# Six PSUM banks in turn, instead of two, for the input products of the first two chunks

## The chip, the cores and the metric

The kernel runs on one core of one Trainium2 chip. The core has a matrix engine (PE, TensorE; its weight loads are the row PEld), a vector engine (DVE), a scalar engine (ACT), a general engine (POOL) and a queue engine (SP) that issues most of the transfers. Each engine works through its own instructions strictly in the order in which they stand in its queue; an instruction waits on semaphores until what it reads is written and what it overwrites is no longer needed. Matrix results land in PSUM, of which this kernel uses eight banks of 128 x 512 float32: one result of 128 x 512 fills one bank, and the bank can take the next result only when DVE or ACT have read the old one.

The metric is the device time of the core in microseconds (us). The kernel before takes 1899.47 us (median of three runs, 1899.46 to 1902.62).

## The reference

The input x has 2048 positions and 1024 channels. Layer 0 is a gated short convolution, layer 1 is stick-breaking attention with 8 heads of 64 channels, and the output is normalised once more. Cut to what matters:

```python
h = _rmsnorm(x, norm_a)                                # mixer (layer 0)
b_gate, c_gate, xin, g = split(h @ w_in, 4)            # w_in: 1024 x 4096
y = b_gate * causal_depthwise_conv(c_gate * xin, w_conv)   # width 3
x = x + (y * silu(g)) @ w_out
k, v = split(_rmsnorm(x, norm_kv) @ w_kv, 2)           # shared keys and values
q, g = split(_rmsnorm(x, norm_b) @ w_in_b, 2)          # layer 1
o = stick_breaking_attention(q, k, v)                  # strictly causal
x = x + (o * silu(g)) @ w_out_b
out = _rmsnorm(x, norm_f)
```

## The kernel before

**Tiling.** The positions are cut into four chunks of 512 (numbered 0 to 3) and the channels into eight blocks of 128. Everything is held transposed, channels on partitions. Each float32 operand of a big product is split into a high part and a low part, and one product of 1024 channels (`mm3`, L202) is 8 x 3 = 24 matmuls of 128 x 128 by 128 x 512, all at line L208, that accumulate into one bank.

**The stage that is changed.** `mixer_in` (L282) computes the products of the mixer's input projection. It is called as `mixer_in((0, 1))` for the first two chunks together and then as `mixer_in((2,))` and `mixer_in((3,))`. For each of the eight column blocks `cb`, and within it for each chunk `c`, it makes four products: C, X, B and G, with tile names pC, pX, pB, pG. What follows each of them on ACT, DVE and POOL:

- pC is copied by ACT to `cs` (L314);
- pX times `cs` gives `p` on DVE (L321), which is scaled by the squared norm factor (L327);
- three convolution steps make `cv` (ACT L334, DVE L335, L337), and DVE multiplies it by pB (L339) and the norm factor (L346);
- pG is scaled (DVE L344), passed through a sigmoid (ACT L345) and multiplied into `cv`, once as the sigmoid (L349) and once as itself (L350); SP stores `cv` to `y_d` (L351).

So pB's bank is free after L339 and pG's bank after L350. The norm factors of the first two chunks are found late, while their first products already run: `rstd` (L119) sums the squares with small matmuls into a bank of its own (`pst`, tag `st`, one buffer), and `bcast` (L143) spreads the result with two matmuls into the same bank (`prb`), from which ACT makes `rs` (L252, L254).

**The banks.** The eight banks are fixed shares of one pool, by tag: `lin` has 2 (L110), `z` 2, `wt` 2, `av` 1 and `st` 1 (L23). Buffers of a tag are reused in turn. All input products take `lin`, but for pB and pG of the very first column block of chunk 0, which take `z`. The attention (`attention`, L466) uses `z` for the scores, `wt` for the transposed weights and `av` for its output.

**Weights.** `load_w` (L183) loads 128 columns of a weight (`wr_`, 512 KB), lets ACT and DVE split them into high and low (`whl_`, L174 and L175), and stores the split form (`sw_`, 1 MB) for the later chunks. There are four `whl` buffers and two raw ones; a weight is split once the same weight of the previous column block has been used by both chunks.

**What runs beside it.** In the same stage `stats_x` (L259) sums the squares of chunks 2 and 3, and `fold_gains` (L355) multiplies `w_kv` and `w_in_b` by their norm gains, in 32 halves: load (L363), DVE multiply (L364), split on ACT (L174) and DVE (L175), two stores (L367), all in the engines' same queues.

**The order.** Python generators yield estimated costs, and `merge` (L672) interleaves the streams by them. A scheduler then puts every engine's instructions in an order of its own by a timeline that it computes when the kernel is built; so a change of buffers can move instructions on every engine. After the first two chunks' mixer follow the output projection and the projections of chunk 0 (`proj_out` L372, products po, then pk, pq, pv, pg) beside the mixer of chunk 2, the attention of chunk 0 and so on; at the end the attention of chunk 3 runs beside the last projections (`out_b`, `out_norm`, `out_b_last`).

Of the kernel before, what the change touches and what calls it, by code (L numbers as in the profile page):

```python
# [8 lines left out]
F32 = mybir.dt.float32  # L9
# [5 lines left out]
P = 128  # L15
# [4 lines left out]
CH = 512  # L20

NR, NW, NT, NL, NWB, NRAW, NA, NWTS = 5, 8, 4, 5, 4, 2, 16, 2
NLIN, NZ, NWT, NAV = 2, 2, 2, 1  # L23
# [22 lines left out]
def kernel(  # L46
# [18 lines left out]
    psum = ctx.enter_context(tc.tile_pool(name="psum", bufs=2, space=bass.MemoryType.PSUM))  # L65
# [43 lines left out]
    def lin(nm):  # L109
        return psum.tile([P, CH], F32, name=nm, tag="lin", bufs=NLIN)  # L110
# [8 lines left out]
    def rstd(acc, nm, y=None):  # L119


        acc = acc if isinstance(acc, (list, tuple)) else [acc]
        ps = st(f"pst_{nm}")
        for j in range(4):
            for i, a in enumerate(acc):
                nc.tensor.matmul(ps[:, j:j + 1], a[:, j * P:(j + 1) * P], ones[:, 0:1], start=i == 0, stop=i == len(acc) - 1)
        v = sb.tile([P, 4], F32, name=f"v_{nm}", tag="sv")
        nc.vector.tensor_scalar(out=v, in0=ps[:, 0:4], scalar1=1.0 / D, scalar2=EPS, op0=ALU.mult, op1=ALU.add)

        if y is None:  # L130
            y = sb.tile([P, 4], F32, name=f"yr_{nm}", tag="sy")
        t = sb.tile([P, 4], F32, name=f"t_{nm}", tag="st")
        nc.vector.tensor_scalar(out=t.bitcast(I32), in0=v.bitcast(I32), scalar1=1, scalar2=None,
                                op0=ALU.logical_shift_right)
        nc.vector.tensor_scalar(out=y.bitcast(I32), in0=t.bitcast(I32), scalar1=-1, scalar2=0x5F3759DF,
                                op0=ALU.mult, op1=ALU.add)
        for _ in range(3):
            nc.vector.tensor_mul(t, y, y)
            nc.vector.scalar_tensor_tensor(out=t, in0=t, scalar=-0.5, in1=v, op0=ALU.mult, op1=ALU.mult)
            nc.vector.scalar_tensor_tensor(out=y, in0=t, scalar=1.5, in1=y, op0=ALU.add, op1=ALU.mult)  # L140
        return y
# [41 lines left out]
    def load_w(src, key, nm, kt=KD, eng=nc.vector):  # L183

        if key not in split_d:
            wt = w_tile(nm, kt)
            raw = sb.tile([P, kt, P], F32, name=f"wr_{nm}", tag="wraw", bufs=NRAW)
            nc.sync.dma_start(out=raw, in_=src.rearrange("(k p) n -> p k n", p=P))
            split(wt[:, 0], wt[:, 1], raw, eng)
            split_d[key] = dram.tile([P, 2, kt, P], F32, name=f"sw_{nm}")  # L190
            nc.sync.dma_start(out=split_d[key], in_=wt.bitcast(F32))
            return wt
        wt = w_tile(nm, kt)
        nc.sync.dma_start(out=wt.bitcast(F32), in_=split_d[key])
        return wt
# [29 lines left out]
    def norm_x_late(c, between=None):  # L225

        hc, xs = [], []
        for k in range(KD):
            if k == 1 and between is not None:
                between()  # L230
            tag, bufs = (("w", NW), ("R", NR) if k < NR else ("ld", NL))[c]
            x = sb.tile([P, CH], F32, name=f"xh_{c}_{k}", tag=tag, bufs=bufs)
            nc.sync.dma_start(out=x, in_=xT[k * P:(k + 1) * P, cols(c)])
            xs.append(x)
            ga = gains["a"][:, k:k + 1]
            hk = act_tile(f"h_{c}", k)
            nc.scalar.activation(hk[:, 0, :], x, AF.Copy, scale=ga)
            nc.vector.scalar_tensor_tensor(out=hk[:, 1, :], in0=x, scalar=ga, in1=hk[:, 0, :].bitcast(F32),
                                           op0=ALU.mult, op1=ALU.subtract)
            hc.append(hk)  # L240
        return hc, xs

    def squares(c, xs):
        acc = sb.tile([P, CH], F32, name=f"acc_h{c}", tag="acc", bufs=2)
        for k, x in enumerate(xs):
            square_into(acc, x, k == 0, f"h{c}{k}", nc.gpsimd, early=True)
        return acc
# [20 lines left out]
    def norm_x(c):  # L268
        hc = []
        pb = bcast(rx[c], f"hb{c}")  # L270
        for k in range(KD):
            x = load_x(c, k, "n")
            nc.vector.scalar_tensor_tensor(out=x, in0=x, scalar=gains["a"][:, k:k + 1], in1=pb,
                                           op0=ALU.mult, op1=ALU.mult)
            hc.append(act_tile(f"h_{c}", k))
            split(hc[k][:, 0, :], hc[k][:, 1, :], x)
        return hc

    h = {}
    late_acc, late = {}, {}  # L280

    def mixer_in(cs):  # L282
        if len(cs) == 1:
            h[cs[0]] = norm_x(cs[0])
            yield YN * 24 * MM
        for cb in range(KD):
            wts = {}
            for c in cs:
                nm = f"{cb}_{c}"

                def w_src(i):
                    return w_in_a[0][:, i * D + cb * P: i * D + (cb + 1) * P]

                def gate(g, i):
                    if c not in h:
                        if c == 0:
                            load_first = lambda: wts.update({g: load_w(w_src(i), (g, cb), f"{g}{cb}_{cs[0]}")})
                            h[c], late_acc[c] = norm_x_late(c, load_first)
                        else:
                            h[c], xs = norm_x_late(c)  # L300
                            late_acc[c] = rstd(squares(c, xs), f"h{c}")
                    if g not in wts:
                        wts[g] = load_w(w_src(i), (g, cb), f"{g}{cb}_{cs[0]}")
                    if c == cb == 0 and g in "BG":

                        ps = psum.tile([P, CH], F32, name=f"p{g}_{nm}", tag="z", bufs=NZ)
                    else:
                        ps = lin(f"p{g}_{nm}")
                    yield from mm3(ps, wts[g], h[c])
                    return ps  # L310

                pc = yield from gate("C", 1)
                cps = t512(f"cs_{nm}")
                nc.scalar.copy(cps, pc)  # L314
                yield rest(24)
                if c == cb == 0:
                    wts["X"] = load_w(w_src(2), ("X", cb), f"X{cb}_{cs[0]}")
                    late_acc[c] = rstd(squares(c, late_acc[c]), f"h{c}")
                px = yield from gate("X", 2)
                p = sb.tile([P, CH + 2], F32, name=f"p_{nm}", tag="p", bufs=2)  # L320
                nc.vector.tensor_mul(p[:, 0:CH], px, cps)  # L321
                pB = None
                if c in late_acc:
                    if c not in late:
                        pB = yield from gate("B", 0)
                        late[c] = late_rms(c, late_acc[c])
                    nc.vector.tensor_mul(p[:, 0:CH], p[:, 0:CH], late[c][1])  # L327
                nc.gpsimd.tensor_copy(p[:, CH:CH + 2], halo[:, cb, :])
                nc.gpsimd.tensor_copy(halo[:, cb, :], p[:, 0:2])
                yield rest(24)  # L330
                if pB is None:
                    pB = yield from gate("B", 0)
                t = t512(f"cv_{nm}")
                nc.scalar.activation(t, p[:, 0:CH], AF.Copy, scale=cw[:, 2, cb:cb + 1])  # L334
                nc.vector.scalar_tensor_tensor(out=t, in0=p[:, 1:CH + 1], scalar=cw[:, 1, cb:cb + 1], in1=t,  # L335
                                               op0=ALU.mult, op1=ALU.add)
                nc.vector.scalar_tensor_tensor(out=t, in0=p[:, 2:CH + 2], scalar=cw[:, 0, cb:cb + 1], in1=t,  # L337
                                               op0=ALU.mult, op1=ALU.add)
                nc.vector.tensor_mul(t, t, pB)  # L339
                yield rest(24)  # L340
                pG = yield from gate("G", 3)
                sg = t512(f"sg_{nm}")
                if c in late:
                    nc.vector.tensor_mul(sg, pG, late[c][0])  # L344
                    nc.scalar.activation(sg, sg, AF.Sigmoid)  # L345
                    nc.vector.tensor_mul(t, t, late[c][1])  # L346
                else:
                    nc.scalar.activation(sg, pG, AF.Sigmoid)
                nc.vector.tensor_mul(t, t, sg)  # L349
                nc.vector.tensor_mul(t, t, pG)  # L350
                nc.sync.dma_start(out=y_d[c][cb], in_=t)  # L351
                yield rest(24)
# [400 lines left out]
```

## Time and profile before

| what | value |
|---|---|
| median of three runs | 1899.47 us |
| the profiled execution: its time | 1899.87 us |
| the profiled execution: its span, first to last instruction | 1898.2 us |
| mean granted PE clock | 0.975 |
| PE busy | 1787.5 us (94%) |
| PEld busy | 1453.6 us (77%) |
| DVE busy | 1264.4 us (67%) |
| ACT busy | 771.9 us (41%) |
| POOL busy | 433.3 us (23%) |
| data moved | 443.65 MB, mean 234 GB/s |

Three views are used below. The **windows** view gives, for stretches of the span, the busy time of each engine with the number of instructions, then the granted PE clock (1.00 is full), the mean busy share of the DMA engines and GB/s. The **timeline** gives instructions in order of time: start, duration, engine, line, operation, output<-inputs, forms and count; where an engine stood idle before the instruction, a bracket gives the idle time and what ended it. The **waits** view sums these idle times by instruction and releaser. Matmuls are pipelined, so their durations overlap: 24 matmuls read as 5.60 us although the next product starts 5.44 us after them. Times between starts are therefore used. Some records may be missing.

### The profile page before, as it was taken

The numbers are of one execution on the slowest core, as the hardware profiler recorded it, in microseconds if no ns is written. First come the engines' busy times: TensorE is split into PE (matmuls) and PEld (weight loads), VectorE is DVE, ScalarE is ACT, GpSimd is POOL, SyncE is SP. The second block draws the span as 40 slices with busy tenths as digits, with TensorE's granted clock in tenths as the row PEclk, the third lists the DMA queues.
The fourth block names the chain that finished last, engine by engine and source line by source line (L and its number), as shares of the span: only waits on it lengthen the run. The fifth ranks groups of instructions, "written<-read, shape, count | busy, mean of one in ns | idle before, by whom it ended". The sixth has DMA issues, their size and how long they took to land.

```text
span 1898.2 us, 24937 instructions
## 1 busy us (share of the span) xinstructions
PE 1787.5 (94%) x8312; PEld 1453.6 (77%) x8312; DVE 1264.4 (67%) x1927; ACT 771.9 (41%) x1497; POOL 433.3 (23%) x822
## 2 busy tenths in 40 slices
PE   7999999999999999999999999999989999888784
PEld 5777888888888878888888888888857777766563
DVE  7766533564133273538886437787996989999996
ACT  6323211231122132325453324444564666566553
POOL 5100000101011031202222102223231323654651
PEclk9999999999999999999999999999989999999797
DMA  9989855697888778776767776656838565777751
GB/s 291 313 293 311 301 154 163 198 355 252 292 270 283 225 261 266 243 266 204 266 214 264 236 253 202 202 191 197 253 104 266 178 195 175 251 252 252 236 170 50
DMA packets 233871, 443.65 MB, mean 234 GB/s; under 512 B 17936, under 2 KB 132624, under 8 KB 209168
## 3 DMA queue, kind: packets, MB, share of 16 engines
q1 hardware_dynamic: 173664, 383.31, 60.1%
q10 hardware_dynamic: 59920, 58.74, 10.7%
q8 instruction: 66, 1.08, 0.2%
q14 instruction: 61, 0.50, 0.1%
q0 software_dynamic: 160, 0.02, 0.1%
HBM read 314.34 MB, written 127.66 MB: 233 GB/s over the span
## 4 chain that ended last, share of the span: by engine, by line
PE 68%; DVE 17%; DMA 6%; issue 5%; ACT 2%; POOL 1%; SPq 0%; ACTq 0%; POOLq 0%; DVEq 0%
PE pX L208 8%; PE pB L208 7%; PE po L208 7%; PE pC L208 7%; PE pG L208 7%; DVE R L501 5%; PE pv L208 4%; PE pk L208 4%; PE wt L513 4%; PE pq L208 4%; PE pg L208 4%; DVE w L505 3%; PE av L523 3%; DVE wtl L175 2%; PE av L522 2%
## 5 line engine op out<-in xcount | busy, mean ns | idle before, releaser
L501 DVE TENSOR_TENSOR_SCAN R<-R,R,ones 128x512 f32<-128x512 f32 x192 | 259.2, 1352 | 23.5 <-ACT R L490 23.2
L490 ACT ACTIVATE R<-z 128x512 f32<-128x512 f32 (+1 forms) x320 | 174.2, 545 | 171.5 <-DVE R L501 80.5
L175 DVE TENSOR_TENSOR wtl<-wt,wth 128x512 fp32r<-128x512 f32 (+1 forms) x320 | 186.2, 600 | 60.7 <-ACT wth L174 60.1
L174 ACT CAST wth<-wt 128x512 fp32r<-128x512 f32 (+1 forms) x320 | 160.6, 528 | 153.2 <-PE wt L513 134.1
L505 DVE TENSOR_TENSOR w<-w,R 128x512 f32<-128x512 f32 (+1 forms) x320 | 209.2, 661 | 16.1 <-POOL R L500 0.5
L208 PE MATMUL pC<-h,whl_C 128*128 128x512 f32 x768 | 193.3, 401 | 14.4 <-ACT whl_C L174 8.2
L208 PE MATMUL pX<-h,whl_X 128*128 128x512 f32 x768 | 188.4, 395 | 5.9 <-DVE cv L350 5.9
L208 PE MATMUL po<-y,whl_o 128*128 128x512 f32 x768 | 187.8, 392 | 0.0
L208 PE MATMUL pB<-h,whl_B 128*128 128x512 f32 x768 | 185.5, 391 | 0.0
L208 PE MATMUL pG<-h,whl_G 128*128 128x512 f32 x768 | 185.0, 391 | 0.0
L500 POOL COPY R<-R 128x1 f32<-128x1 f32 x192 | 103.9, 541 | 349.3 <-DVE R L501 302.2
L208 PEld LDWEIGHTS pC<-h,whl_C 128*128 128x128 f32 x768 | 146.4, 193 | 48.5 <-ACT whl_C L174 8.2
L513 PE MATMUL wt<-ident,w 128*128 128x128 f32 x1088 | 178.5, 279 | 4.3 <-DVE w L505 3.2
L492 ACT ACTIVATE w<-z 128x512 f32<-128x512 f32 (+1 forms) x320 | 171.9, 542 | 6.5 <-PE wt L513 6.5
L208 PEld LDWEIGHTS pX<-h,whl_X 128*128 128x128 f32 x768 | 143.9, 189 | 37.3 <-issue 3.6
L523 PE MATMUL av<-wtl,vv 128*128 128x512 f32 (+1 forms) x320 | 128.9, 405 | 41.5 <-DVE wtl L175 40.1
L208 PEld LDWEIGHTS po<-y,whl_o 128*128 128x128 f32 x768 | 143.1, 188 | 30.2 <-ACT y L174 0.4
L208 PEld LDWEIGHTS pB<-h,whl_B 128*128 128x128 f32 x768 | 143.4, 188 | 29.6
L208 PEld LDWEIGHTS pG<-h,whl_G 128*128 128x128 f32 x768 | 143.3, 188 | 29.7 <-DVE sgb L443 0.2
L513 PEld LDWEIGHTS wt<-ident,w 128*128 128x128 f32 x1088 | 139.7, 144 | 33.1 <-issue 4.2
L501 DVE TENSOR_TENSOR_SCAN R<-R,ones 128x512 f32<-128x512 f32 (+3 forms) x128 | 116.8, 918 | 36.0 <-POOL R L496 32.5
L487 PE MATMUL z<-kt,q 128*128 128x512 f32 (+1 forms) x320 | 129.9, 408 | 7.3 <-ACT w L492 7.1
(170 smaller groups left out, 2676.9 us busy)
## 6 DMA issues: line engine op xcount, KB each, us to landing
whl_o<-sw_o SPq DMA_DIRECT2D x24, 1024.0 KB, 6.1
kt<-k_d ACTq DMA_DIRECT2D x80, 256.0 KB, 4.0
vv<-v_d ACTq DMA_DIRECT2D x80, 256.0 KB, 4.2
whl_C<-sw_C SPq DMA_DIRECT2D x16, 1024.0 KB, 5.9
whl_X<-sw_X SPq DMA_DIRECT2D x16, 1024.0 KB, 5.4
whl_B<-sw_B SPq DMA_DIRECT2D x16, 1024.0 KB, 5.5
whl_G<-sw_G SPq DMA_DIRECT2D x16, 1024.0 KB, 5.3
whl_k<-sw_kv SPq DMA_DIRECT2D x16, 1024.0 KB, 5.6
```

The costliest lines, as they stand in the source:

```text
L174: nc.scalar.copy(hi, src)
L175: eng.tensor_sub(lo, src, hi.bitcast(F32))
L208: ins = nc.tensor.matmul(ps, w[:, k, :], a[k][:, m, :], start=n == 0, stop=n == 3 * kt - 1)
L487: nc.tensor.matmul(ps[:, lom:CH], q2[:, 0, qi * P:(qi + 1) * P], kt[:, lom:CH], start=True, stop=False)
L490: nc.scalar.activation(R[:, lo + 1:CH + 1], ps[:, lo:CH], AF.Sigmoid, scale=-0.125)
L492: nc.scalar.activation(w[:, lo:CH], ps[:, lo:CH], AF.Sigmoid, scale=0.125)
L500: nc.gpsimd.tensor_copy(R[:, 0:1], carry[qi])
L501: nc.vector.tensor_tensor_scan(out=R[:, lo + 1:CH + 1], data0=R[:, lo + 1:CH + 1], data1=ones[:, 0:1].to_broadcast([P, CH - lo]), initial= ...
L505: nc.vector.tensor_mul(w[:, lo:CH], w[:, lo:CH], R[:, lo:CH])
L513: nc.tensor.transpose(wt[:, qi * P:(qi + 1) * P], ws[qi][:, kb * P:(kb + 1) * P], ident)
L522: nc.tensor.matmul(av[:, 0:n], vs, wh[:, 0:n], start=first, stop=False)
L523: ins = nc.tensor.matmul(av[:, 0:n], vs, wl[:, 0:n], start=False, stop=final)
```

## The change

Every input product of the stage for two chunks takes its bank by a running count: `lin`, `z`, `wt`, `lin`, ... and, as each tag has two buffers, a bank comes round again after six products. The special case of the first column block is dropped. The mixers of chunks 2 and 3 keep `lin`.

```diff
     late_acc, late = {}, {}
+    turn = [0]
...
                         wts[g] = load_w(w_src(i), (g, cb), f"{g}{cb}_{cs[0]}")
-                    if c == cb == 0 and g in "BG":
-
-                        ps = psum.tile([P, CH], F32, name=f"p{g}_{nm}", tag="z", bufs=NZ)
+                    if len(cs) > 1:
+
+                        tag, bufs = (("lin", NLIN), ("z", NZ), ("wt", NWT))[turn[0] % 3]
+                        turn[0] += 1
+                        ps = psum.tile([P, CH], F32, name=f"p{g}_{nm}", tag=tag, bufs=bufs)
                     else:
                         ps = lin(f"p{g}_{nm}")
```

The code behind the change stands three lines further down in the new kernel (L350 becomes L353). The lines named here and in the prediction are those of the kernel before.

The order in which the instructions stand on each engine moves with it. PE's order changes in its first 170 groups of matmuls only slightly: a few matmuls of the first block's products are interleaved otherwise, the two `prb` matmuls of chunk 1 now stand after the first six matmuls of the second block's pC instead of before them, and the `pst` sums of chunks 2 and 3 stand up to two blocks later. From there on PE's order is the same up to the attention of the last two heads of chunk 3, the last 270 groups, which are partly interleaved otherwise. DVE, ACT and SP differ through the first five column blocks and then again only in that last part; POOL only in that last part. In the mixer's stage the DVE, ACT and SP queues hold the fold work later: in front of the last step (L350) of chunk 0 in the second block stand six folds' multiplications, not nine. In the last part ACT holds five scalings of an output (`x2r`, L595) further ahead, SP issues the loads of `sga` and `ogr` (L548, L553) further ahead, and DVE the splits of `og` (L175).

## The prediction

> **What bounds the kernel now.** I read the windows of the whole span first, to see where PE, the busiest engine, is not full.
>
> ```profile
> 60.00:230.00 170.00, 159.49 (x689) 130.53 (x688) 108.37 (x179) 49.19 (x73) 7.22 (x16) 0.97 0.91 312
> 230.00:390.00 160.00, 160.00 (x707) 132.51 (x706) 70.62 (x96) 35.26 (x46) 9.06 (x16) 1.00 0.57 177
> 390.00:1400.00 1010.00, 1000.04 (x4789) 829.39 (x4788) 596.18 (x932) 367.11 (x760) 182.98 (x457) 1.00 0.74 244
> 1780.00:1898.00 118.00, 82.07 (x358) 60.77 (x356) 97.98 (x158) 58.88 (x113) 46.89 (x56) 0.85 0.41 131
> ```
>
> From 230 to 1400 us PE sets the pace: 1160 of 1170 us busy, at full clock. Between 60 and 230, inside the changed stage, it loses 10.5 us and some clock. At the end DVE is the fuller engine. The waits of PE between 60 and 230 name what it lacked:
>
> ```profile
> PE pX L208 <- DVE cv L350: 5.9, 3, 3.2
> PE pC L208 <- DVE cv L339: 3.1, 1, 3.1
> PE pst_h L126 <- ACT rs L254: 1.5, 1, 1.5
> ```
>
> L350 and L339 read nothing that pX or pC uses as input; they are the last readers of pG's and pB's banks. These are waits for one of the two `lin` banks; the third is a wait for the `st` bank, which `rs` still reads. The timeline of PE shows their places and what a product takes otherwise:
>
> ```profile
> 62.64 0.63 PE L157 MATMUL prb_h<-dg_h,onesr 128*128 128x512 f32 x2
> 64.82 1.05 PE L126 MATMUL pst_h<-ones,acc_h 128*128 128x1 f32 x8 [1.55 <-ACT rs L254]
> 68.98 8.25 PE L208 MATMUL pC<-h,whl_C 128*128 128x512 f32 x24 [3.11 <-DVE cv L339]
> 77.07 5.60 PE L208 MATMUL pX<-h,whl_X 128*128 128x512 f32 x24
> ...
> 116.10 5.60 PE L208 MATMUL pC<-h,whl_C 128*128 128x512 f32 x24
> 124.90 7.34 PE L208 MATMUL pX<-h,whl_X 128*128 128x512 f32 x24 [3.20 <-DVE cv L350]
> 132.08 5.60 PE L208 MATMUL pB<-h,whl_B 128*128 128x512 f32 x24
> ...
> 164.72 5.60 PE L208 MATMUL pC<-h,whl_C 128*128 128x512 f32 x24
> 171.93 5.69 PE L208 MATMUL pX<-h,whl_X 128*128 128x512 f32 x24 [1.62 <-DVE cv L350]
> 177.46 5.60 PE L208 MATMUL pB<-h,whl_B 128*128 128x512 f32 x24
> ...
> 210.10 5.60 PE L208 MATMUL pC<-h,whl_C 128*128 128x512 f32 x24
> 216.74 5.72 PE L208 MATMUL pX<-h,whl_X 128*128 128x512 f32 x24 [1.04 <-DVE cv L350]
> 222.30 5.60 PE L208 MATMUL pB<-h,whl_B 128*128 128x512 f32 x24
> ...
> 380.06 5.60 PE L208 MATMUL pG<-h,whl_G 128*128 128x512 f32 x24
> 385.50 5.61 PE L208 MATMUL po<-y,whl_o 128*128 128x512 f32 x24
> ```
>
> The last two rows give 5.44 us from product to product (385.50 - 380.06). Four times the stream breaks, always at a block's first or second product, and after the two longer breaks the next product is slow too. From 222 us on no break is left until the stage ends at 385.50.
>
> **The change part by part.** *Removed, the bank waits.* With six banks a product needs the bank of the product six places back. PE then reaches it five products, 5 x 5.44 = 27.2 us, after that one ended, where it was 5.44 us. Why L350 is late I read in DVE's and ACT's timeline:
>
> ```profile
> 120.41 0.69 DVE L364 TENSOR_TENSOR fold_kv<-fold_kv,g_kv 128x512 f32<-128x512 f32 x1 [3.06 <-DMA fold_kv<-in_w_kv_dram]
> 121.02 0.68 DVE L344 TENSOR_TENSOR sg<-pG,rs 128x512 f32<-128x512 f32 x1
> 124.07 0.69 DVE L350 TENSOR_TENSOR cv<-cv,pG 128x512 f32<-128x512 f32 x1
> ```
>
> pG's results were there at 116.10, when the next product began, yet their first reader L344 stands in DVE's queue behind a fold that waits for its load. pG is free at 124.76, 8.66 us after it ended: too late for 5.44 us, early for 27.2. The four breaks, by starts:
>
> - First: 68.98 - 62.64 = 6.34 us, in which prb and pst stand too. Their own cost, which stays, is 0.47 and 0.81 us, from the starts in the rows below. That leaves 5.06. The slow pC took 77.07 - 68.98 = 8.09, that is 2.65 over 5.44.
> - Second: pC should end at 116.10 + 5.44 = 121.54; 124.90 is 3.36 later. pX took 132.08 - 124.90 = 7.18, 1.74 over.
> - Third: 171.93 - 170.16 = 1.77, and 0.09 over in pX.
> - Fourth: 216.74 - 215.54 = 1.20, and 0.12 over.
>
> ```profile
> 390.95 0.62 PE L157 MATMUL prb_hb<-dg_hb,onesr 128*128 128x512 f32 x2
> 391.42 16.50 PE L208 MATMUL po<-y,whl_o 128*128 128x512 f32 x72
> ...
> 446.97 0.95 PE L126 MATMUL pst_x<-ones,acc_x 128*128 128x1 f32 x8
> 447.78 4.61 PE L208 MATMUL pG<-h,whl_G 128*128 128x512 f32 x19
> ```
>
> Waits 5.06 + 3.36 + 1.77 + 1.20 = 11.39, slow products 2.65 + 1.74 + 0.09 + 0.12 = 4.60, together **-15.99 us**. The `st` wait is in it because pst no longer stands between prb and the reading of `rs`, while six matmuls of pC now cover prb's inputs. The price of moving prb: chunk 1's `rs`, and with it its first L327 and the split of whl_G behind it in ACT's queue, come later by the 14 matmuls that now start before prb ends, 14 x 5.44 / 24 = 3.2 us; that eats into the cover below and nothing else.
>
> The slow products are clock: the granted clock was 0.78 and 0.83 in the two windows that hold them.
>
> ```profile
> 70.00:80.00 10.00, 10.00 (x36) 8.03 (x35) 6.50 (x19) 2.37 (x4) 0.00 (x0) 0.78 1.05 356
> 120.00:130.00 10.00, 6.80 (x23) 5.14 (x22) 5.70 (x8) 3.19 (x5) 0.00 (x0) 0.83 1.06 369
> ```
>
> The Trainium skill ("TensorE: Matmul & The Clock Gate", section "Why this matters for your kernels") says that a PE gap of more than about 3 us brings the clock down to half. By that rule the 4.4 us of the first two slow products go away with their gaps, and the 1.77 and 1.20 us gaps cost no clock, as 0.09 and 0.12 show. If the clock fell for another reason, the gain would be 11.4 us and the sum 4.6 us higher.
>
> *What must now keep up: weights.* A product also needs its split weight, and the queues that make it hold the folds too. I set the splits' ends against the products that use them, in the congested block and in a quiet one:
>
> ```profile
> 116.13 1.22 DVE L175 TENSOR_TENSOR whl_B<-wr_B,whl_B 128x1024 fp32r<-128x1024 f32 x1
> 240.44 1.23 DVE L175 TENSOR_TENSOR whl_C<-wr_C,whl_C 128x1024 fp32r<-128x1024 f32 x1 [4.20 <-ACT whl_C L174]
> 254.94 5.60 PE L208 MATMUL pC<-h,whl_C 128*128 128x512 f32 x24
> ```
>
> Quiet: ready at 241.67, used at 254.94, 13.3 us early. Congested: whl_B ready at 117.35, used at 132.08, which is 126.98 once the second break's 5.10 us are gone: 9.6 us early. So folds and transfers delay a split by up to 3.7 us today, of 13.3. Moving the folds back in the order (six, not nine, ahead of L350 in the second block) helps this. Transfers: the stage's bytes stay, so 312 GB/s over 170 us become 312 x 170 / 154 = 344 GB/s; the queue has carried 369 in the window above. I cost the weights at nothing, with 9.6 us of cover; if it is used up, every us more is one of PE's.
>
> *Before 57 us* PE waits for the first inputs; the new interleaving only swaps matmuls that are ready. Nothing. *The banks of the attention*: its first z matmul runs at 514.10, so the tags are free. *From 385 to 1780 us* order and work stay the same, and the rows above show no wait on anything but the core's own progress, so the whole is shifted.
>
> ```profile
> 514.10 0.39 PE L487 MATMUL z<-kt,q 128*128 128x512 f32 x1
> ```
>
> *The last part is reordered.* DVE's work there is the same, and DVE has little to win:
>
> ```profile
> 1780.00:1860.00 80.00, 64.57 (x297) 49.87 (x295) 77.32 (x115) 46.25 (x91) 40.62 (x51) 0.91 0.54 167
> ```
>
> 80 - 77.32 = 2.7 us idle, the bound of a gain. For a loss I take the scalings L595, which in the new order stand ahead of a sigmoid L490 that ran at 1799.92 and feeds the next scan:
>
> ```profile
> 1794.40 11.12 SPq L594 DMA_DIRECT2D x2r<-y_d  x5
> 1799.92 0.60 ACT L490 ACTIVATE R<-z 128x512 f32<-128x512 f32 x1 [0.26 <-PE z L488]
> 1808.77 0.79 ACT L595 ACTIVATE x2r<-x2r,g_f 128x512 f32<-128x512 f32 x1
> ```
>
> If the fifth scaling ended as late as now, 1809.56, the sigmoid would come 9.6 us later: the bound of a loss. But the loads also wait for buffers that the og splits free, and those move forward in the same order, so most of this should not happen. I take +1.0, near the idle time's end of the range.
>
> **Sum.** Against the profiled execution: 1899.87 - 15.99 + 1.0 = 1884.9. That execution is 0.40 over the median of the runs, so **1884.5 us**. Its own range is 1880.8 (tail -2.7) to 1889 (clock not regained, or tail +5.5).
>
> **Rivals.**
>
> *The weights take half of it.* DVE no longer holds PE back, so its backlog of folds reaches the splits, and the second to fourth breaks come back as waits for whl. For it: DVE waits 3.06 us for a fold's load in the row above, and DMA is 0.91 busy. Against it: 9.6 us of cover. The first break stays removed: 1899.5 - 7.7 + 1 = 1892.8 us.
>
> *The tail loses the whole 9.6 us*: 1884.5 + 8.6 = 1893.1 us. For it: SP still issues those loads behind a store and a weight load. Against it: the buffers above.
>
> *The banks do nothing*, if PE waits for DVE some other way, say by `t` buffers of SBUF that hold back the bank's readers: 1899.5. Against: the breaks have a bank's last reader as their releaser, and 27.2 us are a lot.
>
> *Slower: the backlog grows from block to block.* With nothing to slow PE, DVE falls behind further in each block that has folds until a split is more than 13.3 us late; from that point each of six blocks pays a break like the second one, 3.36 + 1.74 = 5.1 us: -16 + 30.6 + 1, or 1915.1 us. Against it: DVE is busy 108 of 170 us, and after 222 us, where today's folds end, it would catch up.
>
> *Slower: the cycling itself costs.* Each product pays for its change of bank: at the first slow product's 2.65 us, 56 products cost 148 us, about 2032 us. The Trainium skill ("TensorE: Matmul & The Clock Gate", section "A second HAM failure mode: psum-queue depth-cycling") reports a kernel whose PE micro-idles and loses clock as it cycles through banks. Here the bank changes with every product already, and 230 to 390 us shows 160.00 of 160 busy at 1.00.
>
> **How the numbers follow.** Chances: forecast 0.74, weights 0.08, tail 0.07, nothing 0.05, backlog 0.05, cycling 0.01. Range: from 1880 (the forecast's lower end) to 1894 (both partial rivals), which leaves out the last three cases. A difference of 0.2%, 3.8 us, is about what can be told from no change: faster than 1895.7 are the first three, 0.89; within it 0.05; slower 0.06.
>
> **What would show it.** Right: PE's timeline from 57 us to the first po holds no wait on L339 or L350 (then L342, L353), products stand 5.44 us apart at clock 1.00, and po starts near 369.5 us instead of 385.50; the first z matmul comes 16 us earlier too. The weights' rival shows as PE waiting for whl_ in that stage; the tail's as a span after 1764 us that is longer than today's 118, with ACT's L490 late behind L595. I would be wrong if po starts early and the attention gives it back before the last heads.

## The result and the profile after

The changed kernel takes 1886.41 us (median of six runs, 1881.34 to 1887.64) against 1899.47 us for the kernel before in the same session (six runs, 1897.79 to 1904.1): 0.9926 of the time, with an interval of 0.9911 to 0.9942. The profiled execution took 1886.36 us with a span of 1884.6 us, 13.6 us less than the 1898.2 us of before. The forecast was 1884.5 us, in a range of 1880 to 1894.

The windows come first, as before: stretch, its length, then busy time and count of PE, PEld, DVE, ACT and POOL, the granted PE clock, the DMA share and GB/s.

```profile
60.00:230.00 170.00, 170.00 (x759) 141.10 (x758) 113.05 (x186) 52.28 (x78) 6.31 (x17) 1.00 0.92 316
230.00:390.00 160.00, 160.00 (x708) 132.55 (x707) 79.47 (x111) 40.53 (x55) 8.94 (x16) 1.00 0.65 209
390.00:1400.00 1010.00, 995.85 (x4762) 826.31 (x4761) 596.57 (x937) 365.88 (x764) 186.73 (x471) 0.99 0.73 240
```

The first row is the change: PE is busy for 170.00 of 170 us at clock 1.00, where it had 159.49 at 0.97. The third row cannot be compared directly: its bounds are fixed in time, the work in it has moved up by 16 us, and so one of the three stretches at half clock in it (at 1393.0 us) belongs to what came after 1400 us before. The other two, at 676.2 and 884.4 us, are a loss. PE's timeline (start, duration, operation, count, and in brackets the idle time before it) shows the stage without its breaks:

```profile
62.49 1.53 PE L208 MATMUL pC<-h,whl_C 128*128 128x512 f32 x6
63.86 0.40 PE L157 MATMUL prb_h<-dg_h,onesr 128*128 128x512 f32 x1
...
66.15 2.43 PE L208 MATMUL pC<-h,whl_C 128*128 128x512 f32 x10
68.42 5.60 PE L208 MATMUL pX<-h,whl_X 128*128 128x512 f32 x24
73.86 5.60 PE L208 MATMUL pB<-h,whl_B 128*128 128x512 f32 x24
...
364.09 5.60 PE L208 MATMUL pG<-h,whl_G 128*128 128x512 f32 x24
369.53 5.61 PE L208 MATMUL po<-y,whl_o 128*128 128x512 f32 x24
```

Products start 5.44 us apart (73.86 - 68.42), and the first po starts at 369.53 us where it was 385.50. The table of PE's waits up to 390 us names no bank and no weight after 57 us; these three rows all belong to the first 57 us:

```profile
PE pC L208 <- ACT whl_C L174: 8.3, 1, 8.3
PE pC L208 <- DVE h L238: 2.2, 3, 0.7
PE prb_h L157 <- DVE dg_h L156: 1.3, 1, 1.3
```

So 16.0 us were won at the front and 13.6 are left at the end. I cut the span at the first and the last po matmul, and add up the time at half clock from the granted clock's record:

```
               first po   to the last po  (half clock)   to the end  (half clock)
before          385.5         997.0           0.0          515.7        83.0
after           369.5         999.6           6.8          515.4        78.6
difference      -16.0          +2.6                         -0.2
```

The missing time is in the middle, beside two stretches at half clock that before did not have.

### The profile page after: what moved, and what is told of

The parts are those of the page before. It is cut to its first block, busy times and chain, and to the rows that moved or that the text cites. A ratio compares the mean times of both kernels' runs of the same rounds, so it can differ in the third digit from the quotient of the medians.

```text
span 1884.6 us, 24926 instructions
## 1 busy us (share of the span) xinstructions
PE 1783.1 (95%) x8312; PEld 1453.1 (77%) x8312; DVE 1264.1 (67%) x1927; ACT 771.9 (41%) x1497; POOL 427.9 (23%) x822
## 4 chain that ended last, share of the span: by engine, by line
PE 74%; DVE 15%; issue 4%; DMA 3%; ACT 2%; POOL 1%; SPq 0%; POOLq 0%; ACTq 0%; DVEq 0%
PE pX L208 9%; PE pC L208 9%; PE pG L208 9%; PE pB L208 9%; PE po L208 8%; DVE R L504 6%; PE pq L208 5%; PE pk L208 4%; PE pv L208 4%; PE wt L516 4%; PE pg L208 4%; DVE w L508 3%; PE av L526 2%; DVE wtl L175 2%; PE av L525 2%
## 5 line engine op out<-in xcount | busy, mean ns | idle before, releaser
L175 DVE TENSOR_TENSOR wtl<-wt,wth 128x512 fp32r<-128x512 f32 (+1 forms) x320 | 186.5, 601 | 65.0 <-ACT wth L174 64.6
L503 POOL COPY R<-R 128x1 f32<-128x1 f32 x192 | 100.0, 521 | 357.4 <-DVE R L504 301.7
```

Source lines behind the costliest of these rows:

```text
L175: eng.tensor_sub(lo, src, hi.bitcast(F32))
L503: nc.gpsimd.tensor_copy(R[:, 0:1], carry[qi])
```

## The experiments

Line numbers in rows are those of the kernel that the row belongs to; in the changed kernel and its variants L339 and L350 stand at L342 and L353 or up to two lines on.

### The changed kernel once more

No edit; the question is whether the middle's loss belongs to the new order or to the execution.

> The changed kernel once more. Two theories of the 3.7 us that the middle lost: two stalls of PE, 1.53 us at 676 us and 1.95 us at 884 us, were each followed by a stretch of 3.41 us at half clock, while the same stalls (1.53 and 1.24 us) in the profile of before cost no clock. Chance: whether a stall of 1 to 2 us costs clock depends on where it falls against something that runs free of the kernel, so this profile shows the same stalls, but the slow stretches elsewhere, more or fewer of them, and the span from the first po to 1400 us differs by a multiple of about 1.7 us. Fixed: the new order makes the stalls fall badly, so the slow stretches stand at 676 and 884 us again, 1.7 us lost at each. Both expect 1886 us within 3, the first po near 369.5 us and no wait for a bank between 57 us and it.

1881.75 us (four runs, 1880.49 to 1884.09), 0.9905 of before (0.9889 to 0.992); first po at 369.2 us; 996.7 us from the first to the last po, with no half clock in it. In the first profile the stall at 676 us looks like this in PE's timeline, with the windows on both sides of 676.2 us below it:

```profile
674.00 0.39 PE L490 MATMUL z<-kt,q 128*128 128x256 f32 x1 [0.70 <-ACT w L495]
674.23 0.28 PE L491 MATMUL z<-kt,q 128*128 128x256 f32 x1
676.03 2.38 PE L208 MATMUL pC<-h,whl_C 128*128 128x512 f32 x5 [1.53 <-DVE cv L342]
```

```profile
672.80:676.20 3.40, 1.17 (x7) 0.69 (x6) 3.40 (x7) 2.47 (x7) 2.05 (x4) 1.00 1.02 303
676.20:679.60 3.40, 3.40 (x9) 2.63 (x10) 3.40 (x6) 0.00 (x0) 2.09 (x4) 0.50 1.06 431
```

In the second execution the same three matmuls stand there with the same two waits, 0.70 and 1.53 us, and the clock stays at 1.00:

```profile
674.08 0.39 PE L490 MATMUL z<-kt,q 128*128 128x256 f32 x1 [0.70 <-ACT w L495]
674.30 0.28 PE L491 MATMUL z<-kt,q 128*128 128x256 f32 x1
676.11 3.24 PE L208 MATMUL pC<-h,whl_C 128*128 128x512 f32 x13 [1.53 <-DVE cv L342]
```

```profile
671.30:674.70 3.40, 2.58 (x13) 1.85 (x11) 3.40 (x7) 2.25 (x6) 1.05 (x5) 1.00 1.01 217
674.70:678.10 3.40, 1.99 (x9) 1.66 (x10) 3.40 (x7) 0.65 (x3) 2.14 (x5) 1.00 1.09 409
678.10:681.50 3.40, 3.40 (x19) 2.92 (x18) 3.40 (x6) 0.13 (x1) 1.11 (x3) 1.00 0.99 403
```

The bounds of these windows are not mine. All half-clock stretches of one execution start at one time plus multiples of 3.413 us, within 2 ns, and that time differs from execution to execution. In the first profile both waits lie in one window of this grid, with 3.40 - 1.17 = 2.23 us of idle time; in the second they are shared out, 0.82 and 1.41 us, as they were before, 1.13 and 1.10. So for this stall the grid alone made the difference. The second stall is another matter, for its length varies too:

```profile
884.17 0.62 PE L526 MATMUL av<-wtl,vv 128*128 128x512 f32 x1 [1.95 <-DVE wtl L175]
```

```profile
881.45 0.50 PE L526 MATMUL av<-wtl,vv 128*128 128x512 f32 x1 [0.77 <-DVE wtl L175]
```

The upper row is the first profile, where the wait of 1.95 us lay in one window (1.45 of 3.40 us busy) and half clock followed; the lower row is the same matmul in the second profile, 0.77 us; in the profile of before it waited 1.24 us. The loss belongs to the execution, and "fixed" is out. Only the profiled executions show where their slow windows lie, so this explains those two spans; that it explains the distance of the two medians, 1886.41 and 1881.75 us, is not shown.

### Four banks

```diff
-    tag, bufs = (("lin", NLIN), ("z", NZ), ("wt", NWT))[turn[0] % 3]
+    tag, bufs = (("lin", NLIN), ("z", NZ))[turn[0] % 2]
```

> Four banks in turn (lin and z), not six. My theory, cover: PE comes back to a bank three products, 16.3 us, after it ended, where the latest reader was 8.66 us late; so four do all that six do: no wait for a bank, first po at 369.5 us within 0.5, time 1886 us within 3. Rival, backlog: DVE's readers fall further behind when nothing slows PE, so that four banks bring part of the breaks back: first po later than 371 us with waits on L342 or L353, and 1888 us or more.

1890.32 us (five runs, 1886.76 to 1895.8), 0.9956 (0.9936 to 0.9977); first po at 373.6 us. Neither forecast: between 60 and 230 us PE is 170.00 us busy, without a wait for a bank, as the cover theory has it, yet the first po comes 4.1 us later than with six. The cause lies ahead of the stage's later blocks, in its start. The first block below is PE's timeline of the start with six banks, the second the same place with four:

```profile
38.65 1.75 PE L208 MATMUL pX<-h,whl_X 128*128 128x512 f32 x7
41.67 0.47 PE L157 MATMUL prb_h<-dg_h,onesr 128*128 128x512 f32 x1 [1.27 <-DVE dg_h L156]
```

```profile
41.68 0.47 PE L157 MATMUL prb_h<-dg_h,onesr 128*128 128x512 f32 x1 [3.44 <-DVE dg_h L156]
```

With six banks matmuls of chunk 1's pX fill part of this place; with four they stand behind prb in PE's order, and the 3.44 us idle are followed by half clock. No bank that is still held explains this: pX of chunk 1 takes the bank of chunk 0's pX, which DVE (L324) read from 28.86 to 29.54 us, and the kernel before, with four banks in its first block too, waits only 1.3 us there. It is the scheduler's order; why it differs stays open. After the start four banks do what six do.

### Six banks in the first block alone

```diff
-    if len(cs) > 1:
+    if len(cs) > 1 and cb == 0:
```

> Six banks in turn for the first block of columns alone, lin's two from the second block on. By my sum the first break (5.06 us of waiting, 2.65 us of slow clock) goes and the other three (6.33 and 1.95 us) stay: first po at 385.5 - 7.7 = 377.8 us, time near 1899.5 - 7.7 + 1 = 1892.8 to 1894.7 us (8.3 over the changed kernel's 1886.4). Rival, one cause: the breaks hang together, and once the first is gone the readers are no longer late, so that the later blocks run free on two banks too: first po near 369.5 and 1886 us. The other rival, the later breaks grow by what the first gives up, since DVE's folds are late by the clock and not by the block: first po near 385.5 and 1899 us.

1891.6 us (ten runs, 1888.69 to 1897.27), 0.9959 (0.9946 to 0.9971); first po at 377.99 us, 7.5 us earlier than before, with three breaks left at the forecast places:

```profile
117.73 5.69 PE L208 MATMUL pX<-h,whl_X 128*128 128x512 f32 x24 [2.52 <-DVE cv L353]
...
163.28 5.72 PE L208 MATMUL pX<-h,whl_X 128*128 128x512 f32 x24 [1.78 <-DVE cv L353]
...
209.22 5.73 PE L208 MATMUL pX<-h,whl_X 128*128 128x512 f32 x24 [2.14 <-DVE cv L353]
```

They sum to 6.44 us, without half clock (before: 3.20, 1.62 and 1.04 us of waiting and 1.95 us of slow clock). The 7.5 us are net of a start that is 0.8 us later (pG at 57.98 us, 57.19 before). Taken alone, from the start of that pG to the block's pX, it is 12.47 us (57.98 to 70.45) against 19.88 before (57.19 to 77.07): the first break is 7.4 us smaller, where I had summed 7.7. It can be had apart from the others, nearly at the price I gave it.

### Six banks from the second block on

```diff
-    if len(cs) > 1:
+    if len(cs) > 1 and cb == 0 and c == 0 and g in "BG":
+        ps = psum.tile([P, CH], F32, name=f"p{g}_{nm}", tag="z", bufs=NZ)
+    elif len(cs) > 1 and cb > 0:
```

> The first block on the banks of the kernel before, six in turn from the second block on. By my sum the first break stays (7.7 us) and the other three go (8.3 us): first po at 385.5 - 8.3 = 377.2 us, time 1886.4 + 7.7 = 1894.1 us within 3. Rival, one cause: with the first break in place nothing else changes order, and the later breaks turn into waits for something else: first po over 380 us and 1897 us or more.

1886.17 us (four runs, 1884.29 to 1887.27), 0.9925 (0.9911 to 0.994): as fast as the changed kernel, 8 us faster than the nearer forecast; first po at 369.71 us. The first break is gone too, with the first block on its old banks. PE's timeline at its place:

```profile
62.67 1.30 PE L208 MATMUL pX<-h,whl_X 128*128 128x512 f32 x5
63.81 0.40 PE L157 MATMUL prb_h<-dg_h,onesr 128*128 128x512 f32 x1
...
68.61 5.60 PE L208 MATMUL pB<-h,whl_B 128*128 128x512 f32 x24
74.05 8.32 PE L208 MATMUL pC<-h,whl_C 128*128 128x512 f32 x36
```

pC's bank comes free later still than before (pB's last reader ends at 73.58 us, at 68.93 before), but pX now has another, and the scheduler puts it and pB ahead of pC. I had priced the break by the bank that was late. It ends as well when any product that is ready has a free bank: the first block's or the next one's will do, and so the two halves of the change do not add up to the whole (7.5 + 15.8 us for 16.0).

### Three banks from the second block on

```diff
+    tags = (("lin", NLIN), ("z", NZ), ("wt", NWT)) if cb == 0 else (("lin", NLIN), ("lin", NLIN), ("z", NZ))
```

> Six banks in turn for the first block, as in the changed kernel, and from the second block on three that matter: lin, lin, z, so that PE comes back to a lin bank two products, 10.9 us, after it ended. The last reader of a lin bank in the changed kernel is at most 9.2 us late after the first block. Cover theory: three are enough by 1.7 us, no wait for a bank from 57 us on, first po at 369.5 us within 0.7, time as with six. Rival, a change of tag as such or the number six counts: a break at the pX of the second, third or fourth block, first po over 371 us.

1884.78 us (four runs, 1882.65 to 1886.49), 0.9908 (0.9893 to 0.9923); first po at 370.11 us. One wait is left:

```profile
206.83 5.68 PE L208 MATMUL pB<-h,whl_B 128*128 128x512 f32 x24 [0.73 <-DVE cv L354]
```

The latest reader of pG in this run ends at 206.68 us, 11.6 us after the next product's start (195.06), which is 0.7 us over the 10.9 of cover: the wait. My bound of 9.2 us for this reader was too low. The number of banks acts through the time that it covers, and three are the edge.

### Two banks, with the folds on GpSimd

The banks are those of "six banks in the first block alone". The edit takes the folds' multiplication and subtraction off DVE, and their copy off ACT.

```diff
-    nc.vector.tensor_mul(raw, raw, gain...)
-    split(hi, lo, raw)
+    nc.gpsimd.tensor_mul(raw, raw, gain...)
+    nc.gpsimd.tensor_copy(hi, raw)
+    nc.gpsimd.tensor_sub(lo, raw, hi.bitcast(F32))
```

> Six banks in the first block and lin's two from the second on, as in the run that kept the three later breaks (waits of 2.52, 1.78 and 2.14 us, first po at 378.0 us), but the folds' three operations run on GpSimd, not on DVE and ACT. If the folds that wait for their loads in DVE's queue make pG's last reader late (7.1 to 7.8 us after pG's end, where blocks without folds have 3.7), it comes 3.7 us after the end again, within the 5.44 us of two banks: the three waits are gone without any further bank, first po at 369.9 us within 1. Rival, the readers' own chain (sigmoid on ACT, four steps on DVE) is too long for two banks wherever the folds run: waits of 1.5 us or more stay at the pX of blocks two to four, first po over 375 us.

1894.11 us (four runs, 1889.16 to 1896.91), 0.9949 (0.993 to 0.9969); first po at 376.84 us, far from the forecast 369.9. Two parts have to be held apart. The start is late, with a wait of its own, and this pG comes 4.6 us later than in the run compared with (57.98 us):

```profile
43.91 0.77 PE L157 MATMUL prb_h<-dg_h,onesr 128*128 128x512 f32 x1 [3.68 <-DVE dg_h L156]
...
62.58 5.61 PE L208 MATMUL pG<-h,whl_G 128*128 128x512 f32 x24
```

From the start of that pG to the first po it takes 376.84 - 62.58 = 314.3 us; with lin's two banks and the folds on DVE it took 320.0 (57.98 to 377.99), with six banks 312.5 (57.05 to 369.53). So the folds' move alone, without a bank, wins back 5.7 of the 7.5 us. Of the three waits the first two are gone and one is left:

```profile
208.10 5.70 PE L208 MATMUL pX<-h,whl_X 128*128 128x512 f32 x24 [1.48 <-DVE cv L353]
```

pG's last readers now come 4.6, 4.9, 6.8 and 4.8 us after the product where the folds on DVE gave 7.8, 7.1, 7.4 and 3.7. The 6.8 belongs to the wait, and DVE's timeline ahead of it, with POOL's below, shows a cost that I had not counted:

```profile
194.93 1.80 DVE L340 SCALAR_TENSOR_TENSOR cv<-p,cw,cv 128x512 f32<-128x512 f32 x1
...
198.16 2.06 DVE L175 TENSOR_TENSOR whl_B<-wr_B,whl_B 128x1024 fp32r<-128x1024 f32 x1
...
205.71 1.53 DVE L352 TENSOR_TENSOR cv<-cv,sg 128x512 f32<-128x512 f32 x1
```

```profile
194.90 1.28 POOL L369 TENSOR_TENSOR fold_b<-fold_b,fold_b 128x512 fp32r<-128x512 f32 x1
197.97 1.18 POOL L367 TENSOR_TENSOR fold_b<-fold_b,g_b 128x512 f32<-128x512 f32 x1 [1.79 <-DMA fold_b<-in_w_in_b_dram]
...
204.72 1.97 POOL L367 TENSOR_TENSOR fold_b<-fold_b,g_b 128x512 f32<-128x512 f32 x1 [2.65 <-DMA fold_b<-in_w_in_b_dram]
```

Each of the three DVE steps overlaps a fold on POOL, and they take 1.80, 2.06 and 1.53 us where the same forms take 0.74, 1.22 and 0.69 when no fold runs on POOL. That the folds in the queues of DVE and ACT make the readers late is shown (which of the two queues does how much is not); that two banks would be enough without them is not, since the folds disturb DVE from POOL too.

### Bare gaps in a stream of matmuls

Two kernels that make no part of the model: groups of matmuls, each waiting for a few steps on DVE. First, short gaps.

> Nothing of the model's computation, only this: 129 groups of 46 to 60 matmuls of 128x512 (10 to 14 us of PE each), each group waiting for one to three steps on DVE that read the group before, so that PE idles between them for eight lengths from about 0.7 to 2.8 us, 16 times each. In the traces so far the half-clock stretches of one run start on one grid of 3.413 us, whose phase differs from run to run, and a grid window in which PE idled over 1.8 us was followed by half clock in 54 of 58 cases, one of under 1.4 us in 10 of 2944. Grid theory: the same here. Gaps under 1.4 us never cost clock; gaps of 1.8 to 2.8 us cost it when most of the gap lies in one window (a 2.2 us gap in about half to two thirds of its 16 cases), each by one window of 3.41 us, and all windows of the run lie on one grid. Rival, a plain threshold on the length of the gap: for each length all 16 cases cost clock or none does, and the slow stretch starts a fixed time after the gap.

The gaps came out at 0.32 to 1.80 us, shorter than planned, and one of 128 cost clock: 1.80 us long, all of it in one window of the grid. This bears out only that short gaps are free, so the gaps were made longer, and the groups too (76 to 90 matmuls, not 46 to 60).

```diff
-KINDS = ((64,), (256,), (512,), (512, 128), (512, 384), (512, 512), (512, 512, 256), (512, 512, 512))
+T3 = (512, 512, 512)
+KINDS = (T3 + (64,), T3 + (256,), T3 + (512,), ... T3 + T3 + (512, 512))
```

> The same bare stream of matmul groups, nothing of the model's computation, with longer gaps: eight lengths from about 1.9 to 4.4 us (the steps that gave 1.71 us plus one to five more, of 0.52 us each), 16 of each, 76 to 90 matmuls between. In the shorter series 127 of 128 gaps (up to 1.80 us) cost no clock; the one that did had all its 1.80 us inside one window of the grid. Grid theory: a gap costs clock when at least 1.8 us of it lie in one window of 3.413 us, so the share of the 16 grows with the length: (1.61 + g - 1.8) / 3.41, about 8 of 16 at 1.9 us, 9 at 2.1, 10 at 2.25, 11 to 12 at 2.6 to 2.8, 15 at 3.3 and all 16 from 3.6 us on; every slow stretch starts on one grid. Rival, a plain threshold on the gap's length, somewhere over 1.8 us: 0 of 16 below it and 16 of 16 above, and the slow stretches start a fixed time after their gap.

Two rows of PE's timeline, behind gaps of the same length:

```profile
143.79 20.73 PE L45 MATMUL ps<-a,identr 128*128 128x512 f32 x83 [2.63 <-DVE a L49]
...
189.12 17.98 PE L45 MATMUL ps<-a,identr 128*128 128x512 f32 x78 [2.63 <-DVE a L49]
```

83 matmuls took 20.73 us, 0.250 each, and 78 took 17.98, 0.231 each. The windows behind the two gaps give the clock, 0.50 and 1.00:

```profile
144.10:147.50 3.40, 3.40 (x9) 2.64 (x8) 0.00 (x0) 0.00 (x0) 0.50 0.00 0
189.10:192.50 3.40, 3.38 (x15) 2.80 (x16) 0.00 (x0) 0.00 (x0) 1.00 0.03 5
```

All gaps between groups:

```
gap, us                1.93  2.03  2.17  2.49  2.63  3.09  3.55  4.01
number                   17    16    16    16    16    15    16    16
followed by half clock    7     4     6     7    13    12    14    16
```

The share rises with the length, if not from each column to the next, where a threshold on the length would give none or all; and all stretches start on one grid. By the largest part of a gap that lies in one grid window: none of those below 1.87 us cost clock, all of those over 1.94 did, and between them 9 of 13. The bound is nearer 1.9 us in this run than the 1.8 that I put in the expectation (the one case of the shorter series was at 1.80). The expectation forecast too many for the first three columns, 8 to 10 of 16; the bound is one reason, but with 1.9 in its formula it would still give about 8, so the rest is how these gaps happened to fall.

## Why the prediction was right

**The bank waits, -11.39 us, and the slow products, -4.60.** Together -15.99 us were forecast at the first po; it came 385.50 - 369.53 = 15.97 us earlier, of which 0.14 is a pG that starts earlier (57.05 us, 57.19 before). The clock was regained in full: the stage has 1.00 in both windows. The forecast's cause, folds ahead of pG's readers in DVE's queue, is borne out by the folds' move, which took them off ACT's queue too. The cover is borne out by its dose: two banks (5.44 us) leave waits of 2.52, 1.78 and 2.14 us, three (10.9 us) one of 0.73, four and six none after the start.

**The first break** was nearly right in size (7.4 us for 7.7) and too narrow in its cause. I had one bank and the `st` bank to blame; the run with the old banks in the first block shows that PE only needed one ready product with a bank of its own.

**The price of moving prb**, 3.2 us for chunk 1's `rs`: L252 ran at 66.35 us where it had run at 63.70, 2.65 us later, and PE did not wait for anything behind it.

**The weights at nothing** held: no whl_ in PE's waits after 57 us. The two rivals that start there, half of the gain and a growing backlog, are out, and so is the one in which the banks do nothing. But the cover shrank more than I had allowed. The folds did not move up with the products: the last one stands on DVE at 217.83 us, 3.6 us earlier than before (221.41), while the products come 16 us earlier; and the transfers did not go up to my 344 GB/s (316 between 60 and 230 us). So DVE falls behind a little when nothing slows PE. From the second block on, the latest reader of pG ends 8.7 us after the start of the next product in the kernel before, 8.9 us after it in the changed kernel and 11.6 in the run with three banks; the tightest split ended 8.1 us ahead of its product (whl_G, 160.14 for 168.25) and in the second profile 6.8 (whl_B, 242.64 for 249.48), where the narrowest of my estimate was 9.6. My count of folds' multiplications ahead of L350 of chunk 0 in the second block was off as well: DVE's trace has eleven before and seven after, not nine and six; the direction is the same.

**The cycling rival** is out: clock 1.00 and 170.00 of 170 us busy with a bank that changes at every product, over six banks.

**"From 385 to 1780 us order and work stay the same, so the whole is shifted"** is the step that failed, by 2.6 us. Order and work did stay, but the waits did not all, and their place on the clock's grid did not. The waits of 0.70 and 1.53 us are there in every profile and cost clock when both fall into one window; the wait for `wtl` at 884 us was 1.24 us before, 1.95 and 0.77 in the two profiles after. PE's idle time in this stretch rose by only 0.5 us (6.3 against 5.8); most of the loss is the clock. Over eight profiles (before, the changed kernel twice, and five variants) the stretch from the first to the last po took 996.5 to 997.2 us with no half clock in it, 998.4 us with one window of 3.41 us, and 999.5 or 999.6 with two: about 1.4 to 1.7 us each. What I used as a bound, gaps of 1.77 and 1.20 us that cost no clock, was true of these two and no rule. I leaned on the Trainium skill ("TensorE: Matmul & The Clock Gate", section "Why this matters for your kernels") and its 3 us; here the runs differ, and 1.95 us of idle time, in one wait, were enough when they fell in one window.

**The tail, +1.0 us**: from the last po to the end it took 515.7 us before, 515.4 after and 513.8 in the second profile of the changed kernel. The reordering cost nothing that could be told from the spread (514.4 to 522.0 us in the variants); the rival with 9.6 us is out. The +1.0 that did not come stood in for part of the middle's 2.6: against the profiled execution -15.0 us were forecast and -13.6 measured, and without it the sum would have been 1.0 us further off. That is luck.

So 1884.5 us stands between the two sessions' medians, 1886.41 and 1881.75 us, and what separates these two is not in the kernel's text: in the profiles, 3.0 of the 5.0 us are the middle with and without its two slow windows, and 1.6 are the tail, where the clock is unsteady in every run.

## What to carry to other kernels

When the matrix engine waits for a bank, compare how late the bank's last reader is with the number of products that the banks let pass meanwhile; three banks covered 10.9 us here, against readers that were 8 to 12 us late, and more than that bought 0.7 us. A free bank also gives the scheduler something to put ahead of a late product, so where the banks stand matters less than that one ready product has one. Price a stall of PE together with its neighbours, as idle time per stretch of 3.4 us: here less than some 1.8 us cost itself alone, and more than some 1.9 us cost about 1.4 to 1.7 us of clock on top. In the last 500 us of the model less was enough at times, as the next section shows.

## What the hardware showed beside

**The clock's grid.** In each of the eight profiles of the whole model the half-clock stretches start on one grid of 3.413 us, within 2 ns, whose phase changes with every execution, and last one, two or three such windows; only the last one, as the kernel ends, runs on. From 57 us on the eight profiles hold 4,083 windows at full clock. Of these, all 75 in which PE idled over 1.8 us were followed by half clock, 19 of 37 with 1.6 to 1.8 us, 6 of 37 with 1.4 to 1.6 and 12 of 3,934 with less. (By the same count the six profiles of the expectation above have 60 such windows, all followed by half clock, where it says 54 of 58.) Up to 1370 us the line is sharp: no window with 1.78 us or less was followed by half clock, and every one from 1.79 us on was. The mixed cases all stand later, where the idle time alone does not decide; what else does stays open. The Trainium skill ("TensorE: Matmul & The Clock Gate", section "Part 1: The HAM clock gate (the "warmup" mystery)") describes a free-running window of 3413 ns; the traces agree with the window, and not with its table, which names at least one idle window of about 3.4 us.

**At half clock it is harder to come back.** In the same profiles, from 57 us on and the final stretch of each left out, all 50 half-clock windows with 0.6 us or more of idle time were followed by another one, and 98 of the 103 with less than 0.2 us were the last of their stretch.

**GpSimd slows DVE.** With the folds on POOL, DVE steps of 128x512 or more that overlap them take up to 2.4 times as long (1.80 us for 0.74), as the rows above show. Not every step does: from 60 to 246 us the 19 that read a product out of PSUM (L324, L342, L347, L353) and lay for more than half of their time beside a fold took 0.69 us each, as they do alone; the slowed ones had both inputs in SBUF.
